# The gates of a DeltaNet layer: weights as the moving operand, tokens as the stationary one

## The chip, the cores and the metric

The kernel runs on one core of a Trainium2 chip. Its time is that of one execution on the device in microseconds; the median of the runs is compared. Below, PE is TensorE (matmuls; PEld is the loading of its stationary operand), DVE is VectorE, ACT is ScalarE, POOL is GpSimd and SP is the queue that issues the DMAs.

## What is computed

Two decoder layers on 1024 tokens of 1024 channels, in float32. The first has a gated DeltaNet as its token mixer, the second a convolution module; behind each is an MLP. Only the start of the DeltaNet matters here:

```python
proj = h @ w_in                                   # h: 1024 tokens x 1024; w_in: 1024 x 4112
qkv, z, bt, at = split(proj, [3072, 4096, 4104])  # bt, at: 8 columns each, one a head
qkv = silu(causal_depthwise_conv(qkv, conv_w))
beta = sigmoid(bt)
g = -exp(a_log) * softplus(at + dt_bias)
o = gated_delta_rule(l2norm(q), l2norm(k), v, g, beta)   # chunks, head by head
```

The gates bt and at are 16 columns of 4112. Everything in the delta rule waits for them: beta scales the Gram matrix of the keys, the running sum of g gives every decay.

## The kernel before

**Precision.** A float32 matmul is made of three in the faster fp32r format: each operand is split into a high part, rounded by a cast, and a low part, the rest. `mm3` issues high x high, high x low and low x high into one PSUM bank. A weight tile `raw` of 128x1024 is loaded by SP, its high part `whi` is cast on ACT (line 412, 225 in the first stage), its low part `wlo` is subtracted on DVE (line 415, 227). The input h is kept as H[half][k]: high and low part of 128 channels (block k) by 512 tokens (a half).

**A dense tile.** 128 output channels by 512 tokens: for each of 8 blocks of channels `mm3` takes a 128x128 weight block as the stationary operand and 512 tokens as the moving one, so 24 matmuls of 512 columns (lines 234 to 236). Tokens end up along the free axis.

**The first stage** (lines 287 to 305) fills all eight PSUM banks at once for the first half of the tokens, while the vectors of the conditioning are still being computed: for each k, h's block is made and multiplied by eight weight tiles from one load of 1024 columns, `w_first`. Bank 0 is the gates, padded from 16 to 128 columns with zeros; banks 1 to 7 are k, q, v of head 0, k, q, v of head 1 and k of head 2. The engines' order here is left to the framework's scheduler.

**The order behind it is written by hand.** For PE, DVE and ACT each piece of work is a generator, and a list of numbers says at which time (in slots, one a head, about 29 us) each of its steps is emitted. All steps are sorted by these times, and each of the three engines runs its instructions strictly in that order; a step that waits holds all behind it on its engine. POOL and SP are ordered by the scheduler. A weight tile's load, cast and subtraction get their times from the tile ahead of it: `tile_events` takes three times from the list `last` and leaves three for the next tile.

**The gates.** `token_gates(0)` takes bank 0: ACT copies 16 rows of it (line 354), four transposes (line 358) bring tokens onto the partitions, and DVE and ACT compute beta and the decays; two small products with a triangle give the running sums (lines 388, 389), one row a head goes to DRAM and comes back broadcast over all partitions. The second half's gates are a dense tile of their own in slot 7: 512 KB of weights loaded, cast and subtracted, 24 matmuls between times 7.0 and 7.2, then the same steps.

**PSUM.** In this part there are two banks for each of four tags: pd (dense tiles), pp (small products of a head's preparation and of the gates), pi (inverse), ps (scan). Who takes a bank with a tag waits until one is free, that is until all readers of the tile in it have run.

**What runs around time 7.** The steps of one head u are at fixed offsets:

- `head_prep` at u + 1: transposes of k into a pp bank at -0.0922 (line 493); ACT squares them at -0.0063 (line 496); the Gram product takes a pp bank at 0.0109 (line 501); DVE reads that at 0.1551 (line 512, writes NT); ACT reads the transposes again at 0.1822 (line 522, writes kd); the transposes of q take a pp bank at 0.2501 (line 527).
- `head_decay` at u: the exponentials of the decay on ACT at 1.1256 (lines 476, 477).
- `head_scan` at u + 3: a product on PE at 0.0646 (line 678), its reader on DVE at 0.0737 (line 681), then PE at 0.1923 (lines 685 to 689).
- `conv`, behind a projection tile: ACT copies and scales at 0.04 (lines 434, 439), three DVE steps (line 442), SiLU on ACT (line 445).

So at time 7 head 6 is in preparation and head 4 begins its scan.

Of the kernel before, what the change touches and what calls it, by code (L numbers as in the profile page):

```python
# [9 lines left out]
F32 = mybir.dt.float32  # L10
# [6 lines left out]
P = 128  # L17
D = 1024
# [37 lines left out]
DNO_AT = 0.0843  # L56
OG_AT = 4.8655
LATE_AT = (18.6148, 20.1732)
G0_AT = (-1.8, -1.7, -0.06, -0.01, 0.09, 0.25, 0.62, 0.645, 0.7, 0.72)
FIRST_AT = (  # L60
    (-1.6, -0.165, -0.12, -0.07, 0.1), (-1.2, -0.012, 0.03, 0.08, 0.11), (-0.02, 0.13, 0.175, 0.2, 0.27),
    (0.13, 0.49, 0.51, 0.53, 0.58), (0.25, 0.6, 0.65, 0.7, 0.74), (0.57, 0.75, 0.8, 0.85, 0.9),
# [1 line left out]
)  # L64
W_FIRST = ((-2.3, -1.95, -1.9),)
H0_AT = (0.8992, 1.98, 2.4218, 2.6956, 3.874, 4.2736, 6.2935, 6.8047)
G1_AT = (-0.0095, 0.088, 0.1601, 0.2135, 0.3241, 0.487, 0.7341, 0.7578, 1.2185, 1.3557)
PLAN = {
    0: (0, 3, ()), 1: (4, 1, ()), 2: (1, 2, ()), 3: (0, 2, ()), 4: (3, 0, ()), 5: (3, 0, ()), 7: (4, 0, ()), 8:
    (4, 0, ()), 14: (2, 1, ()), 15: (2, 1, ()), 16: (0, 2, ()), 17: (0, 2, (3,)), 18: (0, 0, (6, 0, 4, 7, 1)),  # L70
# [53 lines left out]
def tile_hybrid(ctx, tc, xT, c, adaT, cols, rows, gates, w_gate, w_first, w_dn, w_dno, w_cf, w_cfo,  # L124
# [39 lines left out]
    def bank(tag):  # L164
        return banks["pool"].tile([P, HALF], F32, name=nm(tag), tag=tag, bufs=banks[tag])
# [3 lines left out]
    def blk(j):  # L169
        return slice(j * P, (j + 1) * P)  # L170
# [16 lines left out]

    def raw_tile(ap):
        raw = wb("raw", 1024)
        nc.sync.dma_start(raw, ap)  # L190
        return raw

    def ada(l, j, k, raw=None):
# [27 lines left out]

    def load_w(ap):
        raw = raw_tile(ap)
        hi = wb("whi", 1024, F32R)
        sc.copy(hi, raw)
        lo = wb("wlo", 1024, F32R)
        ve.tensor_tensor(lo, raw, hi.bitcast(F32), op=ALU.subtract)
        return hi, lo

    def mm3(ps, w, off, acts, first=True, last=True):  # L230
# [53 lines left out]


    sb = Bufs("start", raw=6, tz=6)
    first = [bank(t) for t in ("pd", "pd", "pp", "pp", "pi", "pi", "ps", "ps")]
    for k in range(KT):
        ada(0, 1, k, sb("raw", D))
        ada(0, 0, k, sb("raw", D))  # L290
# [44 lines left out]
    gp.memset(W64, 0.0)  # L335
    beta, gam, negam, kdec, gdr = {}, {}, {}, {}, {}

    def v3(t):
        return t.rearrange("p (c m) -> p c m", m=P)

# [5 lines left out]

    def token_gates(hf):

        if hf == 0:
            ps = first[0]  # L350
        else:
            ps = yield
        gt = hb("tz")
        sc.copy(gt[0:16, :], ps[0:16, :])
        yield
        gps = bank("pp")
        for j in range(NC2):
            te.transpose(gps[:, j * 16:(j + 1) * 16], gt[0:16, blk(j)], ident[0:16, 0:16])
        yield
        gv = gps[:, 0:64].rearrange("p (c t h) -> p t h c", t=2, h=NH)  # L360

        def tile_(name):
            return dp(f"{name}{hf}", [NH, NC2])

        b_, gx, gy, gz, gq, gcol = [tile_(n) for n in ("beta", "gx", "gy", "gz", "gq", "gcol")]
        ve.tensor_tensor(gx, gv[:, 1], gate_c[:, 1, :].unsqueeze(2).broadcast_to(GS), op=ALU.add)
        yield

        sc.activation(gy, gx, AF.Abs)
        sc.activation(gy, gy, AF.Exp, scale=-1.0)  # L370
        sc.activation(b_, gv[:, 0], AF.Sigmoid)
        yield
        ve.tensor_scalar(gz, gy, 2.0, None, op0=ALU.add)
        yield
        ve.reciprocal(gz, gz)
        ve.tensor_mul(gy, gy, gz)
        ve.tensor_mul(gz, gy, gy)
        ve.tensor_scalar(gq, gz, 2.0 / 19.0, None, op0=ALU.mult)
        for t_ in range(17, 1, -2):
            ve.scalar_tensor_tensor(gq, gq, 2.0 / t_, gz, op0=ALU.add, op1=ALU.mult)  # L380
        ve.scalar_tensor_tensor(gq, gq, 2.0, gy, op0=ALU.add, op1=ALU.mult)
        ve.scalar_tensor_tensor(gq, gx, 0.0, gq, op0=ALU.max, op1=ALU.add)
        ve.tensor_tensor(gcol, gq, nea.unsqueeze(2).broadcast_to(GS), op=ALU.mult)
        yield

        n = NH * NC2
        ps = bank("pp")
        te.matmul(ps[:, 0:n], lhsT=kc[:, K_TRI, :], rhs=flat(gcol), start=True, stop=True)
        te.matmul(ps[:, n:2 * n], lhsT=kc[:, K_STR, :], rhs=flat(gcol), start=True, stop=True)
        yield  # L390
        gm, ng, kd = [tile_(x) for x in ("gam", "negam", "kdec")]
        ve.tensor_copy(flat(gm), ps[:, 0:n])
        sc.activation(flat(kd), ps[:, n:2 * n], AF.Exp)
        sc.activation(ng, gm, AF.Exp)
        yield
        ve.tensor_scalar(ng, ng, -1.0, None, op0=ALU.mult)
        ps = bank("pp")
        te.transpose(ps[0:n, 0:P], flat(gm), ident)
        yield
        grow = dp("grow", P, p=n)  # L400
        ve.tensor_copy(grow, ps[0:n, 0:P])
        d = dr.tile([NH, HALF], F32, name=nm("gdr"))
        nc.sync.dma_start(d.rearrange("h (c p) -> (h c) p", p=P), grow)
        beta[hf], gam[hf], negam[hf], kdec[hf], gdr[hf] = b_, gm, ng, kd, d
        yield
# [321 lines left out]
    def add(lab, g, *times):  # L727
        for t_ in times:
            events.append((t_, len(events), lab, g))
# [25 lines left out]
        tile_events(f"z{hf}", w_dn[24 + h], hf, t0, dur, lambda d: z_out(d, h, hf), Z_AT)  # L755

    def gate_events(t0, dur):
        g = token_gates(1)
        d = {}

        def post(d):
            g.send(None)
            g.send(d["ps"])
            yield
            yield from g

        tile_events("gates1", w_gate, 1, t0, dur, post, *G1_AT)

    def x_new(k):
        need("h", 0, k, n=2)  # L770
# [12 lines left out]
    order[6:12] = [(2, "k"), (2, "q"), (3, "k"), (3, "q"), (2, "v"), (3, "v")]  # L783
    for i, (u, t_) in enumerate(order[:7]):
        nt = {"q": 0, "k": 8, "v": 16}[t_] + u % NH
        add(f"proj0{u}", conv({"ps": first[1 + i]}, nt, 0, t_, heads[u]), *FIRST_AT[i])
    plan = {t_: PLAN.get(t_, (3, 0 if t_ < 12 else 1, ())) for t_ in range(19)}
    done = 7
    zs = 0
# [460 lines left out]
def layout(x, c, ada_w, ada_b, ln_g, ln_b, dn_w_in, dn_conv_w, dn_a_log, dn_dt_bias,  # L1250
           dn_norm_w, dn_w_out, cf_w_in, cf_dw_w, cf_dw_b, cf_ln_g, cf_ln_b, cf_w_out, ff_w1, ff_w2):
    cols = np.concatenate([
        _cols(ada_b), _cols(ln_g), _cols(ln_b),
        dn_conv_w[0].reshape(CONV, 24, P).transpose(2, 1, 0).reshape(P, 96),
        dn_norm_w[0][:, None],
        cf_dw_w[0].reshape(CFK, KT, P).transpose(2, 1, 0).reshape(P, KT * CFK),
        _cols(cf_dw_b), _cols(cf_ln_g), _cols(cf_ln_b)], axis=1)
    wg = np.zeros((D, P), np.float32)
    wg[:, :16] = dn_w_in[0][:, 4096:4112]
    return {  # L1260
        "xT": x[0].T.reshape(KT, P, S),
        "c": c,
        "adaT": ada_w.transpose(0, 2, 1).reshape(2, 48, P, D),
        "cols": cols,
        "rows": np.stack([ln_g[1, 1], ln_b[1, 1]]),
        "gates": np.stack([dn_a_log[0], dn_dt_bias[0]]),
        "w_gate": _wtiles(wg)[0],
        "w_first": np.concatenate([wg] + [dn_w_in[0][:, n * P:(n + 1) * P] for n in (8, 0, 16, 9, 1, 17, 10)],
                                  axis=1).reshape(KT, P, 1024),
        "w_dn": _wtiles(dn_w_in[0][:, :4096]),  # L1270
        "w_dno": _wtiles(dn_w_out[0]),
        "w_cf": _wtiles(cf_w_in[0]),
        "w_cfo": _wtiles(cf_w_out[0]),
        "w_1": np.stack([_wtiles(w) for w in ff_w1]),
        "w_2": ff_w2.reshape(2, 8, 4, P, 4, 2, P).transpose(0, 1, 4, 3, 5, 2, 6).reshape(2, 8, 4, P, 1024),
        "consts": _consts(),
    }
# [18 lines left out]
```

## Time and profile before

| | us |
|---|---|
| median of 3 runs (lowest, highest) | 2411.41 (2410.13, 2414.36) |
| the profiled execution | 2410.48 |
| its span in the profile | 2408.6 |
| first stage, until the gates' transposes | 57.35 |
| gates' tile of the second half | 254.97 to 260.78 |

The span is that of the instructions; the execution's own time has 1.9 us around it. A record of PE is longer than the time until the next one starts, since matmuls are pipelined: the pace is read from the starts. The granted clock of PE is 1.00 at 2.4 GHz and 0.50 at 1.2 GHz.

### The profile page before, as it was taken

Reading aid. Unit: us, or ns where it says so; the run is one execution under the profiler, and the core shown is the slowest. Engines: PE = TensorE matmul, PEld = TensorE weight load, DVE = VectorE, ACT = ScalarE, POOL = GpSimd, SP = SyncE. Lnnn points to the kernel's source line nnn. Section 1 sums busy time; section 2 is a strip of 40 time slices with the busy share of each in tenths; the row PEclk is TensorE's granted clock in tenths of the full one; section 3 lists DMA queues with packets and bytes.
Section 4 is the critical chain, followed back from the end, with each engine's and each line's share of the span. In section 5 each row is a group of like instructions: output and inputs, shape, how many; then the busy total and the mean of one; then the engine's idle time right before and its main releaser. Section 6 shows DMA issues by size and latency. Waiting matters only on the chain.

```text
span 2408.6 us, 33443 instructions
## 1 busy us (share of the span) xinstructions
PE 2357.5 (98%) x12730; PEld 1946.2 (81%) x12730; DVE 1722.9 (72%) x2712; ACT 1100.3 (46%) x1949; POOL 409.3 (17%) x841
## 2 busy tenths in 40 slices
PE   8899999999999999999999999999999999999998
PEld 6677878787778888888888888878888888888887
DVE  6667677676686566656899998799888766444447
ACT  4767767564256333335433334563333336333333
POOL 1356556454410000000000001100000001000003
PEclk9999999999999999999999999999999999999999
DMA  8343223334553556542322222222222332222223
GB/s 303 107 131 100 87 66 86 102 102 137 188 159 104 171 186 197 191 155 88 105 97 96 97 96 96 97 97 104 97 96 96 101 118 97 96 97 96 96 97 131
DMA packets 118143, 287.02 MB, mean 119 GB/s; under 512 B 35168, under 2 KB 44768, under 8 KB 117984
## 3 DMA queue, kind: packets, MB, share of 16 engines
q1 hardware_dynamic: 117984, 284.90, 36.3%
q8 instruction: 100, 1.64, 0.3%
q14 instruction: 59, 0.48, 0.1%
HBM read 275.35 MB, written 9.50 MB: 118 GB/s over the span
## 4 chain that ended last, share of the span: by engine, by line
PE 80%; DVE 7%; POOL 5%; DMA 4%; ACT 2%; issue 2%; SPq 0%; DVEq 0%; ACTq 0%; POOLq 0%
PE pd L234 25%; PE pd L236 25%; PE pd L235 24%; POOL T L563 2%; POOL X L565 2%; PE pp L982 1%; DVE wlo L415 1%; DVE tl L1031 1%; DVE lo L246 1%; DVE tl L1033 1%; DMA A<-d_in 1%; DMA d_in<-NT 1%; DMA Xc<-d_out 1%; DVE ax L259 1%; DVE raw L202 1%
## 5 line engine op out<-in xcount | busy, mean ns | idle before, releaser
L234 PE MATMUL pd<-hh,whi 128*128 128x512 f32 x2014 | 817.9, 406 | 6.9 <-DVE ax L259 3.9
L236 PE MATMUL pd<-hh,wlo 128*128 128x512 f32 x2014 | 789.5, 392 | 1.9 <-DVE wlo L415 1.8
L235 PE MATMUL pd<-lo,whi 128*128 128x512 f32 x2014 | 788.4, 391 | 0.6 <-DVE lo L246 0.6
L412 ACT CAST whi<-raw 128x1024 fp32r<-128x1024 f32 x382 | 398.4, 1043 | 544.5 <-PE pd L235 535.1
L415 DVE TENSOR_TENSOR wlo<-raw,whi 128x1024 fp32r<-128x1024 f32 x382 | 468.1, 1226 | 25.9 <-ACT whi L412 23.6
L236 PEld LDWEIGHTS pd<-hh,wlo 128*128 128x128 f32 x2014 | 379.6, 189 | 85.8 <-DVE wlo L415 4.7
L234 PEld LDWEIGHTS pd<-hh,whi 128*128 128x128 f32 x2014 | 381.4, 189 | 78.7 <-issue 3.9
L235 PEld LDWEIGHTS pd<-lo,whi 128*128 128x128 f32 x2014 | 381.6, 189 | 69.7 <-DVE lo L246 1.8
L234 PE MATMUL pd<-xh,whi 128*128 128x512 f32 (+1 forms) x1056 | 404.9, 383 | 0.0
L235 PE MATMUL pd<-xl,whi 128*128 128x512 f32 (+1 forms) x1056 | 404.1, 383 | 0.3 <-DVE xl L246 0.3
L236 PE MATMUL pd<-xh,wlo 128*128 128x512 f32 (+1 forms) x1056 | 404.1, 383 | 0.0
L961 DVE SCALAR_TENSOR_TENSOR cv<-u,col,cv 128x512 f32<-128x512 f32 x480 | 359.1, 749 | 9.6 <-ACT cv L957 1.8
L259 DVE SCALAR_TENSOR_TENSOR ax<-pd,mod,ax 128x512 f32<-128x512 f32 x280 | 208.4, 749 | 154.0 <-PE pd L236 152.9
L246 DVE TENSOR_TENSOR xl<-ts,xh 128x512 fp32r<-128x512 f32 x128 | 88.4, 691 | 256.6 <-ACT ts L905 256.0
L899 ACT ACTIVATE tz<-pd 128x512 f32<-128x512 f32 x128 | 76.6, 599 | 394.9 <-PE pd L236 394.9
L235 PEld LDWEIGHTS pd<-xl,whi 128*128 128x128 f32 x1056 | 198.5, 188 | 39.3 <-DVE xl L246 0.5
L234 PEld LDWEIGHTS pd<-xh,whi 128*128 128x128 f32 x1056 | 198.6, 188 | 38.6
L236 PEld LDWEIGHTS pd<-xh,wlo 128*128 128x128 f32 x1056 | 198.5, 188 | 38.5
L202 DVE CUSTOM_DVE_ANT_0 raw<-raw,condb 128x1024 f32<-128x1024 f32 x96 | 117.9, 1229 | 24.1 <-DMA raw<-in_adaT_dram 23.9
L563 POOL TENSOR_TENSOR T<-X,A 32x15 f32<-32x15 f32 (+7 forms) x240 | 100.1, 417 | 23.9 <-DMA A<-d_in 5.8
L565 POOL TENSOR_TENSOR X<-X,T 32x15 f32<-32x15 f32 (+7 forms) x240 | 99.1, 413 | 18.3
L991 POOL TENSOR_SCALAR lnst<-mv 128x1 f32<-128x1 f32 x32 | 14.9, 465 | 508.6 <-DVE mv L990 338.7
(248 smaller groups left out, 2177.5 us busy)
## 6 DMA issues: line engine op xcount, KB each, us to landing
raw<-in_w_dram SPq DMA_DIRECT2D x260, 512.0 KB, 3.2
raw<-in_adaT_dram SPq DMA_DIRECT2D x96, 512.0 KB, 3.4
raw<-in_w_dn_dram SPq DMA_DIRECT2D x57, 512.0 KB, 3.8
raw<-in_w_cf_dram SPq DMA_DIRECT2D x32, 512.0 KB, 3.2
raw<-in_w_dno_dram SPq DMA_DIRECT2D x16, 512.0 KB, 3.3
raw<-in_w_cfo_dram SPq DMA_DIRECT2D x16, 512.0 KB, 3.2
raw<-in_w_first_dram SPq DMA_DIRECT2D x8, 512.0 KB, 6.5
tz<-in_xT_dram SPq DMA_DIRECT2D x16, 256.0 KB, 5.5
```

The costliest lines, as they stand in the source:

```text
L202: ve.tensor_tensor_reduce(out=raw, in0=raw, in1=condb, op0=ALU.mult, op1=ALU.add, scale=1.0, scalar=0.0, accum_out=mod[l][j][:, k:k + 1])
L234: te.matmul(ps, lhsT=w[0][:, s_], rhs=ah, start=(first and i == 0), stop=False)
L235: te.matmul(ps, lhsT=w[0][:, s_], rhs=al, start=False, stop=False)
L236: te.matmul(ps, lhsT=w[1][:, s_], rhs=ah, start=False, stop=(last and i == n - 1))
L246: ve.tensor_tensor(lo, x32, hi.bitcast(F32), op=ALU.subtract)
L259: ve.scalar_tensor_tensor(AX[hf][k], ps, g[:, k:k + 1], AX[hf][k], op0=ALU.mult, op1=ALU.add)
L412: sc.copy(hi, raw)
L415: ve.tensor_tensor(lo, raw, hi.bitcast(F32), op=ALU.subtract)
L563: gp.tensor_tensor(t, X[:, 0:i + 1, i:i + 1].broadcast_to(sh), A[:, i:i + 1, i + 1:].broadcast_to(sh), op=ALU.mult)
L565: gp.tensor_tensor(X[:, 0:i + 1, i + 1:], X[:, 0:i + 1, i + 1:], t, op=ALU.subtract)
L899: sc.activation(r, d[0], AF.Relu)
L961: ve.scalar_tensor_tensor(cv, u[:, j:j + HALF], col[:, b_ + j:b_ + j + 1], cv, op0=ALU.mult, op1=ALU.add)
```

## The change

The gates' products are turned round: 128 tokens of h are the stationary operand, and the 16 weight columns of the gates the moving one. For each of four blocks of tokens and each of eight blocks of channels there are two products: h's high part with 32 columns (high and low weights side by side), and h's low part with the 16 high columns. That is 64 narrow products a half, into one bank of which 128 columns are used; tokens come out on the partitions, so the transposes go. ACT copies the one half of the columns to SBUF, and DVE adds the other. The weights (64 KB) are loaded, cast and subtracted once, behind the first stage.

The first stage fills seven banks from loads of 896 columns. Its narrow products for the first half stand at -0.013 to -0.01, ahead of the first dense tile, into a ps bank. Those of the second half stand at 7.06, 7.10, 7.14 and 7.18, into a pp bank; the dense tile in slot 7 is gone, and the slot is still divided by five. The gates' Exp and Sigmoid in the first half move from -0.01 to 0.11, behind the SiLU of head 0's k (0.10) and q (0.11).

```diff
-G0_AT = (-1.8, -1.7, -0.06, -0.01, 0.09, 0.25, 0.62, 0.645, 0.7, 0.72)
+G0_AT = (-0.013, -0.012, -0.011, -0.01, 0.1, 0.11, 0.16, 0.25, 0.62, 0.645, 0.7, 0.72)
-G1_AT = (-0.0095, 0.088, 0.1601, 0.2135, 0.3241, 0.487, 0.7341, 0.7578, 1.2185, 1.3557)
+G1_AT = (-0.14, -0.1, -0.06, -0.02, 0.03, 0.08, 0.2, 0.3241, 0.7341, 0.7578, 1.2185, 1.3557)
...
-    first = [bank(t) for t in ("pd", "pd", "pp", "pp", "pi", "pi", "ps", "ps")]
+    first = [bank(t) for t in ("pd", "pd", "pp", "pp", "pi", "pi", "ps")]
...
+    wg, raw_g = dp("wg", [KT, 32], F32R), hb("tz")
+    nc.sync.dma_start(raw_g[:, 0:P], w_gate)
+    raw_g = raw_g[:, 0:P].rearrange("p (k n) -> p k n", k=KT)
+    sc.copy(wg[:, :, 0:16], raw_g)
+    ve.tensor_tensor(wg[:, :, 16:32], raw_g, wg[:, :, 0:16].bitcast(F32), op=ALU.subtract)
...
     def token_gates(hf):
-        if hf == 0:
-            ps = first[0]
-        else:
-            ps = yield
-        gt = hb("tz")
-        sc.copy(gt[0:16, :], ps[0:16, :])
-        yield
-        gps = bank("pp")
-        for j in range(NC2):
-            te.transpose(gps[:, j * 16:(j + 1) * 16], gt[0:16, blk(j)], ident[0:16, 0:16])
-        yield
-        gv = gps[:, 0:64].rearrange("p (c t h) -> p t h c", t=2, h=NH)
+        gps = bank("pp" if hf else "ps")
+        for j in range(NC2):
+            for k in range(KT):
+                need("h", hf, k, n=1)
+                hi, lo = H[hf][k]
+                te.matmul(gps[:, j * 32:(j + 1) * 32], lhsT=hi[:, blk(j)], rhs=wg[:, k], start=(k == 0), stop=False)
+                te.matmul(gps[:, j * 32:j * 32 + 16], lhsT=lo[:, blk(j)], rhs=wg[:, k, 0:16], start=False,
+                          stop=(k == KT - 1))
+            yield
+        gs = dp("gs", [NC2, 16])
+        gv = gps[:, 0:NC2 * 32].rearrange("p (c n) -> p c n", c=NC2)
+        sc.copy(gs, gv[:, :, 16:32])
+        ve.tensor_tensor(gs, gs, gv[:, :, 0:16], op=ALU.add)
+        gv = gs.rearrange("p c (t h) -> p t h c", t=2)
...
     def gate_events(t0, dur):
-        g = token_gates(1)
-        d = {}
-
-        def post(d):
-            g.send(None)
-            g.send(d["ps"])
-            yield
-            yield from g
-
-        tile_events("gates1", w_gate, 1, t0, dur, post, *G1_AT)
+        add("gates1", token_gates(1), *[t0 + dur + o for o in G1_AT])
...
-        add(f"proj0{u}", conv({"ps": first[1 + i]}, nt, 0, t_, heads[u]), *FIRST_AT[i])
+        add(f"proj0{u}", conv({"ps": first[i]}, nt, 0, t_, heads[u]), *FIRST_AT[i])
```

`load_w` and `raw_tile` take tiles narrower than 1024 columns, and the host lays out the 16 gate columns alone and seven tiles in `w_first`.

## Rows read from the trace of the kernel before

**Rows 1.** The page, busy time of the engines, share of the span, instructions.
```profile
PE 2357.5 (98%) x12730; PEld 1946.2 (81%) x12730; DVE 1722.9 (72%) x2712; ACT 1100.3 (46%) x1949; POOL 409.3 (17%) x841
```
**Rows 2.** Windows: stretch, length, busy of PE, PEld, DVE, ACT, POOL, clock, DMA.
```profile
250.00:300.00 50.00, 48.85 (x368) 39.91 (x367) 33.26 (x82) 35.74 (x90) 23.78 (x59) 1.00 0.34 102
300.00:350.00 50.00, 47.16 (x426) 37.76 (x425) 39.23 (x85) 34.31 (x95) 27.04 (x55) 1.00 0.27 79
...
800.00:900.00 100.00, 100.00 (x443) 82.84 (x442) 64.38 (x100) 37.02 (x51) 0.57 (x3) 1.00 0.58 190
```
**Rows 3.** Timeline of PE, 254 to 262 us: start, duration, instruction, idle before.
```profile
254.16 1.06 PE L501 MATMUL pp<-k 128*128 128x128 f32 x8
254.97 0.48 PE L234 MATMUL pd<-hh,whi 128*128 128x512 f32 x1
...
257.11 0.38 PE L678 MATMUL ps<-lo,ax 128*128 128x128 f32 x2
...
260.78 0.38 PE L685 MATMUL ps<-vt,ax 128*128 128x128 f32 x2
```
**Rows 4.** Timeline of PE, 57 to 58.6 us.
```profile
57.35 0.41 PE L358 MATMUL pp<-ident,tz 16*128 16x16 f32 x4
57.69 0.50 PE L234 MATMUL pd<-hh,whi 128*128 128x512 f32 x1
```
**Rows 5.** Timeline of PE, 134.9 to 140 us.
```profile
136.02 1.00 PE L642 MATMUL pi<-V64T,NT 128*128 128x64 f32 x8
136.83 0.48 PE L234 MATMUL pd<-hh,whi 128*128 128x512 f32 x1
```
**Rows 6.** Timeline of PE, 292 to 297 us.
```profile
293.58 0.31 PE L388 MATMUL pp<-gcol,kcl 128*128 128x32 f32 x2
...
293.94 0.48 PE L234 MATMUL pd<-hh,whi 128*128 128x512 f32 x1
```
**Rows 7.** Timeline of DVE, 44 to 56 us.
```profile
50.44 1.23 DVE L227 TENSOR_TENSOR wlo<-raw,whi 128x1024 fp32r<-128x1024 f32 x1 [0.25 <-ACT whi L225]
```
**Rows 8.** Timeline of all engines, 60 to 115 us: TensorE.
```profile
65.35 0.74 PE L234 MATMUL pd<-hh,whi 128*128 128x512 f32 x1 [1.91 <-ACT whi L412]
...
68.49 0.57 PE L234 MATMUL pd<-hh,whi 128*128 128x512 f32 x1
```
**Rows 9.** Timeline of ACT, 50 to 66 us.
```profile
59.37 1.28 ACT L371 ACT_TABLE_LOAD   x1
```
**Rows 10.** Timeline of DVE, 253 to 264 us.
```profile
257.53 0.35 DVE L681 TENSOR_SCALAR vt<-ps,br 128x128 f32<-128x128 f32 x1 [4.56 <-PE ps L678]
...
261.49 1.13 DVE L512 SCALAR_TENSOR_TENSOR NT<-pp,br,ax 128x128 f32<-128x128 f32 x4
```
**Rows 11.** Waits of PE: who waited for whom, total, times, longest.
```profile
PE pp L527 <- DVE NT L512: 1.2, 2, 0.7
```
**Rows 12.** Timeline of ACT, 253.5 to 264 us.
```profile
254.98 0.73 ACT L439 ACTIVATE v<-pd,col 128x512 f32<-128x512 f32 x1
258.46 1.06 ACT L412 CAST whi<-raw 128x1024 fp32r<-128x1024 f32 x1 [2.75 <-DMA raw<-in_w_dn_dram]
259.53 1.28 ACT L476 ACT_TABLE_LOAD   x1
...
261.88 1.12 ACT L522 ACTIVATE ax<-pp,kdec 128x128 f32<-128x128 f32 x4
```
**Rows 13.** Windows of PE: stretch, length, busy, granted clock, DMA.
```profile
120.50:126.50 6.00, 5.98 (x76) 0.50 0.44 119
```
**Rows 14.** Timeline of PE, 108 to 128 us.
```profile
120.52 0.65 PE L598 MATMUL pi<-Tb,NT 32*32 32x32 f32 x32 [2.52 <-DVE Tb L583]
```
**Rows 15.** Timeline of PE, 698 to 714 us.
```profile
707.30 1.91 PE L982 MATMUL pp<-ident,ax 128*128 128x128 f32 x8
...
712.48 1.03 PE L982 MATMUL pp<-ident,ax 128*128 128x128 f32 x8
```
**Rows 16.** Groups of instructions of the whole span: busy, mean ns, idle before.
```profile
L234 PEld LDWEIGHTS pd<-hh,whi 128*128 128x128 f32 x2014 | 381.4, 189 | 78.7 <-issue 3.9 <-ACT whi L412 3.6 <-ACT whi L225 1.2
```

More of the change, by code (lines that the diff above doesn't have):

```diff
@@ L189, in raw_tile @@
         raw = wb("raw", 1024)
-        nc.sync.dma_start(raw, ap)
+        nc.sync.dma_start(raw[:, 0:ap.shape[-1]], ap)
         return raw
@@ L223, in load_w @@
         raw = raw_tile(ap)
+        n = ap.shape[-1]
         hi = wb("whi", 1024, F32R)
-        sc.copy(hi, raw)
+        sc.copy(hi[:, 0:n], raw[:, 0:n])
         lo = wb("wlo", 1024, F32R)
-        ve.tensor_tensor(lo, raw, hi.bitcast(F32), op=ALU.subtract)
+        ve.tensor_tensor(lo[:, 0:n], raw[:, 0:n], hi[:, 0:n].bitcast(F32), op=ALU.subtract)
         return hi, lo
@@ L1257, in layout @@
         _cols(cf_dw_b), _cols(cf_ln_g), _cols(cf_ln_b)], axis=1)
-    wg = np.zeros((D, P), np.float32)
-    wg[:, :16] = dn_w_in[0][:, 4096:4112]
     return {
@@ L1266, in layout @@
         "gates": np.stack([dn_a_log[0], dn_dt_bias[0]]),
-        "w_gate": _wtiles(wg)[0],
-        "w_first": np.concatenate([wg] + [dn_w_in[0][:, n * P:(n + 1) * P] for n in (8, 0, 16, 9, 1, 17, 10)],
-                                  axis=1).reshape(KT, P, 1024),
+        "w_gate": dn_w_in[0][:, 4096:4112].reshape(KT, P, 16).transpose(1, 0, 2).reshape(P, P),
+        "w_first": np.concatenate([dn_w_in[0][:, n * P:(n + 1) * P] for n in (8, 0, 16, 9, 1, 17, 10)],
+                                  axis=1).reshape(KT, P, 7 * P),
         "w_dn": _wtiles(dn_w_in[0][:, :4096]),
```

## The prediction

> **What bounds the kernel now.** I read the page first. TensorE is busy for almost the whole span [rows 1]. Its record overstates it (matmuls are pipelined), so the second view is busy time by stretches: after the DeltaNet part TensorE has no gap at all, while in the DeltaNet part VectorE and ScalarE are at two thirds to four fifths and TensorE has 1 to 3 us of gap in 50 us [rows 2]. The reader is to see that a microsecond of TensorE work added or taken in the DeltaNet part mostly reaches the end, because the engines run in a written order and everything behind moves with it; only a gap that lies behind the change can swallow some. The third view is the timeline at the two places where the gates are computed: the end of the first stage (50 to 72 us) and slot 7 (254 to 266 us).
>
> **What the change takes away.** The first stage loses one bank of eight: 8 blocks of 3 products. The gates' tile of the second half is the same 24 products: in slot 7 they stand between 254.97 and 260.78, with the two short products of line 678 among them, 5.8 us in all, or 0.23 us a product [rows 3]. So 5.5 us of TensorE work go from each place, and with them the four transposes, 0.34 us (57.35 to 57.69) [rows 4].
>
> **What it adds.** 64 products a half, each with its own 128x128 stationary tile and 32 or 16 moving columns. No row has this form in fp32r. The nearest: eight products of line 642 (64 columns, full stationary tile) run from 136.02 to 136.83, 0.101 us each [rows 5]; four with 32 columns from 293.58 to 293.94, 0.09 us each [rows 6]; four transposes with 16 columns on 16 rows in 0.34 us, 0.085 us each [rows 4]. A quarter fewer columns change little, so the loading of the stationary tile sets the pace and not the columns. I take 0.10 us: 6.4 us a half (5.4 at 0.085; 6.9 at 0.107, were the load alone a little slower). Against 5.8 us with the transposes this is +0.6 us a half. The narrow form does not save TensorE work.
>
> The Trainium skill (TensorE: Matmul & The Clock Gate, section Back-to-back issue gap) gives about 81 ns for a sustained pair of load and matmul at 128 columns; by it the 64 would take some 5.2 us, an estimate. The eight of line 642 run at 101 ns here, so the row is used. The same page (Part 3, The mechanism) says that a weight load overlaps a running matmul only if the row groups differ; by that 64 products would take a load and a stream each.
>
> **Place 1, the first stage and gates0.** The stage ends today at 57.35 [rows 4], behind a backlog of products. Without 5.5 us of them it would end at 51.8; VectorE's last low part ends at 51.67 [rows 7], is an eighth shorter in each of eight blocks (0.15 us of 1.23, so 1.2 us earlier in all: 50.5), and seven products of 0.23 us follow: 52.1. From there 6.4 us of narrow products give 58.5, so the first dense tile starts 0.8 us later than at 57.69. What follows is set by ScalarE: the second tile waits 1.91 us for its cast and then runs at the lower clock until 68.5 [rows 8]. The evacuations of the seven banks move forward under the narrow products and shorten that wait. But the gates' Exp and Sigmoid now stand behind the SiLU of head 0's k and q, where they stood ahead of them: two more table loads of 1.28 us [rows 9]. Bounds: the wait and its slow stretch vanish, -1.9 and -1.5 us (half of the 3.1 us that were slow); or nothing of it vanishes and the delay and both loads land on the path, 0.8 + 2.6 = +3.4 us. I take 0, for both sides are as large.
>
> The narrower casts, the half megabyte less in the first loads and the 64 KB of the gates' weights cost nothing that I count: they lie under the stage's products. If the cover goes, the copy and subtraction of the small weights are two instructions of 128 elements a row, some 0.35 us each by line 681 [rows 10].
>
> **Place 2, slot 7.** Here the order changes. The four blocks of narrow products stand at 7.06, 7.10, 7.14 and 7.18, and the first takes a bank with the tag pp, of which there are two. At 7.06 both are held by the preparation of head 6: the bank of the k transposes (taken at 6.908, read last by line 522 at 7.182) and that of the Gram product (line 501 at 7.011, read by line 512 at 7.155). That such a hold stops TensorE shows in the wait of line 527 for line 512, the reader of the bank before it [rows 11]. Which of the two comes free first? Line 512 stands on VectorE behind line 681 at 7.074, and that waits for line 678 at 7.065, which now stands behind the narrow products on TensorE [rows 10]. So VectorE can't free one, and line 522 on ScalarE must. ScalarE ends the convolution's copies at 255.71; it then waited 2.75 us for a weight tile and cast it, the tile after the gates' [rows 12]. In the changed order that tile takes over the early load and cast of the gates' tile (the list of times handed from tile to tile has one member less), so ScalarE goes on at once: table load, two exponentials, line 522, which took from 259.53 to 263.00, 3.47 us [rows 12]. The bank is free at about 259.2. TensorE has done line 501 at 254.97 and has nothing in between, for the dense tile that stood there is gone: it stands still for 4.2 us. Then 6.4 us of narrow products and the 0.14 us of line 678 end at 265.75, where line 685 now starts at 260.78 [rows 3]: +5.0 us. Queued behind: lines 678, 681, 512, hence head 6's solve, and the next dense tiles.
>
> A stop of that length has a second price. After a stop of 2.52 us the granted clock stood at 0.50, the lower level of 1.2 GHz, for 6.0 us [rows 13, 14]; after the one of 1.91 us products ran slow for 3.1 us [rows 8]. That costs half of it with dense products behind, 1.5 to 3 us. Here narrow ones follow; eight transposes took 1.91 us at the lower level and 1.03 at the higher [rows 15], so if all 64 run slow it is about 0.8 x 6.4 = 5.1 us, and 3 us more for dense ones behind. I take 3 us, with 0 and 8 as ends.
>
> The gates' load of 512 KB, its cast and its subtraction leave SP, ScalarE and VectorE in this slot. I count nothing for it: TensorE, which waits for none of them there today, is what ends last. Of the gaps behind the place, 2.8 us between 300 and 350 [rows 2], some may swallow a little; I take none off.
>
> **Sum.** 0 + 5.0 + 3 = +8 us. The profiled execution took 2410.48 us, 1.9 us more than its span, and the median of the runs is 0.9 us above it. On the execution 2418.5; on the runs 2419.
>
> **The rivals.**
> *The bank is not late.* If ScalarE is far enough ahead, or the reader of the other bank goes first, only the added work is left, 2 x 0.6 us, and place 1: +1 to +3 us, 2413. For it speaks that ScalarE sat idle for 2.75 us in this very place; against it that its chain to line 522 starts only when the preceding dense tile is done.
> *Faster.* The DeltaNet part hangs on the chain through ScalarE, VectorE and GpSimd, not on TensorE. That chain begins with the evacuation of the first stage's banks, and the stage ends at 52.1 in place of 57.35: everything behind comes 5.2 us earlier, and in slot 7 TensorE's stop is slack, since the chain waits for line 522 as before: -5.2 us, 2406. It decides if less than 0.4 us of the 5.2 is lost on the way, for 4.8 us are 0.2%. For it speaks that TensorE stood behind ScalarE at 65.35 [rows 8] and has gaps all through the part [rows 2]; against it that these gaps are only 1 to 3 us in 50.
> *The narrow runs are slow themselves.* TensorE falls to the lower clock in the narrow run of place 1 too, or each product pays load and stream one after the other: 64 x 0.08 = 5 us and 1.5 to 3 of dense ones behind it, on top of the forecast and with the whole 8 in slot 7: +8 + 5 + 5 = +18 us, 2429. No row shows a run of narrow products longer than 1 us, so nothing excludes the first. The second the Trainium skill's rule on overlap would bring; the trace speaks against it: a load is recorded with 0.19 us [rows 16], and line 642 starts a product each 0.101.
>
> **How the numbers follow.** The forecast has 0.55 (by itself 2414 to 2426), the bank that is not late 0.23, faster 0.09, the slow narrow runs 0.13. Of the forecast about a tenth falls within 0.2% (4.8 us, about what a measurement of this kernel tells from no change), because gaps behind may swallow part. Slower 0.62, the same 0.29, faster 0.09. The range is 2409 to 2428: it leaves out the faster case and the upper end of the slow runs.
>
> **What would show it.** Right: between line 501 of head 6 and the first narrow product TensorE is idle for some 4 us, released by ScalarE's line 522, with a granted clock near 0.5 just behind; the narrow products start 0.09 to 0.11 us apart at the full clock; the first stage ends near 52; the first dense tile starts at 58 to 59. Wrong: TensorE goes from line 501 straight into narrow products; or they stand 0.06 or 0.2 us apart; or the delay of slot 7 is gone again by 350 us, swallowed by gaps.

## The result: 0.8% slower, and the profile after

The changed kernel took 2432.0 us (median of 4 runs, 2426.4 to 2432.6) against 2412.2 us for the kernel before on the same chip: ratio 1.0079, 95% interval 1.0067 to 1.0091. The forecast was 2419, its range ended at 2428. Of the rivals, that of the slow narrow runs (2429) came nearest; how far its reasons hold is told further down. The profiled executions stand 21.1 us apart (2431.62 and 2410.48).

The page's busy times hide this: TensorE is busy for the same 98% as in [rows 1], with 72 instructions more and 13.9 us more busy time.

```profile
PE 2371.4 (98%) x12802; PEld 1961.5 (81%) x12802; DVE 1721.1 (71%) x2714; ACT 1098.4 (45%) x1949; POOL 407.8 (17%) x841
```

To see where the time went I lay one instruction that every head has once, the Gram products (line 501 before, 510 after), side by side in the two timelines. Head 0 starts 3.1 us later than before, head 6 4.1 us, head 7 18.3 us, head 15 22.3 us. So in these two executions the first place costs 3 to 4 us, slot 7 costs 14.2 us, and 3.3 us come between heads 8 and 9. Lines after the edit have moved: 234 is now 235, 501 is 510, 522 is 531, 678 is 687, 685 is 694; the narrow products are lines 361 (high part, 32 columns) and 362 (low part, 16).

Head 7's Gram products, first before, then after (head 6's are in [rows 3] and below):

```profile
296.08 1.06 PE L501 MATMUL pp<-k 128*128 128x128 f32 x8
```
```profile
314.39 1.05 PE L510 MATMUL pp<-k 128*128 128x128 f32 x8
```

The first place, timeline of TensorE in the kernel after: start, duration, instruction. It answers to [rows 4] and [rows 8].

```profile
52.83 0.39 PE L237 MATMUL ps<-hh,wlo 128*128 128x512 f32 x1
53.06 0.18 PE L361 MATMUL ps<-wg,hh 128*128 128x32 f32 x1
...
57.66 0.26 PE L361 MATMUL ps<-wg,hh 128*128 128x32 f32 x1
57.77 0.27 PE L362 MATMUL ps<-wg,lo 128*128 128x16 f32 x1
57.90 0.38 PE L361 MATMUL ps<-wg,hh 128*128 128x32 f32 x1
58.11 0.36 PE L362 MATMUL ps<-wg,lo 128*128 128x16 f32 x1
...
61.95 0.36 PE L362 MATMUL ps<-wg,lo 128*128 128x16 f32 x1
62.16 0.77 PE L235 MATMUL pd<-hh,whi 128*128 128x512 f32 x1
...
67.86 0.52 PE L236 MATMUL pd<-lo,whi 128*128 128x512 f32 x1
68.22 0.40 PE L237 MATMUL pd<-hh,wlo 128*128 128x512 f32 x1
```

No line here has a bracket, so TensorE waited for nothing. The products start 0.111 us apart until 57.77 and 0.213 us apart from 57.90: in the middle of the run, 4.8 us after its start, the clock fell to the lower level. The run took 9.1 us, and the dense products behind it stayed slow until 67.9. The windows say the same: full busy, granted clock 0.79, then 0.50 (1.2 GHz). Columns: stretch, length, TensorE busy, granted clock, DMA share and GB/s.

```profile
55.00:60.00 5.00, 5.00 (x38) 0.79 0.02 7
60.00:65.00 5.00, 5.00 (x18) 0.50 0.00 0
...
260.00:265.00 5.00, 1.68 (x8) 0.77 0.81 227
265.00:270.00 5.00, 5.00 (x25) 0.50 0.28 110
270.00:275.00 5.00, 5.00 (x25) 0.50 0.25 59
275.00:280.00 5.00, 5.00 (x51) 0.50 0.00 0
280.00:285.00 5.00, 5.00 (x20) 0.68 0.01 2
```

The lower five are slot 7: the clock is down for some 19 us. The timeline of TensorE there, beside [rows 3]:

```profile
258.24 1.06 PE L510 MATMUL pp<-k 128*128 128x128 f32 x8
263.32 0.40 PE L361 MATMUL pp<-wg,hh 128*128 128x32 f32 x1 [4.02 <-ACT ax L531]
263.56 0.36 PE L362 MATMUL pp<-wg,lo 128*128 128x16 f32 x1
...
266.76 0.77 PE L687 MATMUL ps<-lo,ax 128*128 128x128 f32 x2
...
277.42 0.77 PE L694 MATMUL ps<-vt,ax 128*128 128x128 f32 x2
...
279.14 0.80 PE L235 MATMUL pd<-hh,whi 128*128 128x512 f32 x1
...
283.39 0.40 PE L236 MATMUL pd<-lo,whi 128*128 128x512 f32 x1
```

The stop is in the bracket: 4.02 us, released by the copies that read the k transposes' bank. All 64 narrow products behind it stand 0.213 us apart, from 263.3 to 277.4, and the full rate is back only at 283.4, behind dense products. ScalarE went on without the wait of [rows 12], as the prediction had it, from line 448 into the table load:

```profile
259.06 0.72 ACT L448 ACTIVATE v<-pd,col 128x512 f32<-128x512 f32 x1
259.80 1.28 ACT L485 ACT_TABLE_LOAD   x1
...
262.15 1.12 ACT L531 ACTIVATE ax<-pp,kdec 128x128 f32<-128x128 f32 x4
```

### The profile page after: what moved, and what is told of

It is laid out like the page before. It is cut to its first block, busy times and chain, and to the rows that moved or that the text cites. A ratio compares the mean times of both kernels' runs of the same rounds, so it can differ in the third digit from the quotient of the medians.

```text
span 2429.7 us, 33585 instructions
## 1 busy us (share of the span) xinstructions
PE 2371.4 (98%) x12802; PEld 1961.5 (81%) x12802; DVE 1721.1 (71%) x2714; ACT 1098.4 (45%) x1949; POOL 407.8 (17%) x841
## 4 chain that ended last, share of the span: by engine, by line
PE 80%; DVE 8%; POOL 5%; DMA 3%; ACT 2%; issue 2%; SPq 0%; ACTq 0%; DVEq 0%; POOLq 0%
PE pd L235 24%; PE pd L237 24%; PE pd L236 24%; POOL T L572 2%; POOL X L574 2%; PE pp L982 1%; DVE wlo L424 1%; DVE raw L202 1%; DVE lo L247 1%; DMA Xc<-d_out 1%; DVE tl L1031 1%; DVE tl L1033 1%; DVE ax L260 1%; DMA raw<-in_adaT_dram 1%; PE ps L687 0%
## 5 line engine op out<-in xcount | busy, mean ns | idle before, releaser
L574 POOL TENSOR_TENSOR X<-X,T 32x15 f32<-32x15 f32 (+7 forms) x240 | 96.2, 401 | 18.3
```

The costliest lines, as they stand in the source:

```text
L574: gp.tensor_tensor(X[:, 0:i + 1, i + 1:], X[:, 0:i + 1, i + 1:], t, op=ALU.subtract)
```

## The experiments

Each kernel is compared with the kernel before on the same chip. That took 2410.9 us beside half0, half1, bank_pd and wide, 2411.4 beside wide_pd, mix, two and stop_dense, and 2413.4 beside wide_pd2 and two2. The table shows, for the profiled execution of each kernel, how much later than before the Gram products of head 0, head 6 and head 7 start, worked out from the timelines; the last column is the difference of the two before it, the price of slot 7 in that execution. The kernel half0, whose slot 7 is that of before, shows 1.2 us there: smaller differences say nothing. A profiled execution can lie some us off the median of its kernel (bank_pd 2427.2 against 2422.8, wide_pd2 2423.6 against 2418.3), and the changed kernel's began its products 0.8 us earlier than that of the kernel before. So the columns of head 0 and head 6 are rough; slot 7 is a difference within one execution, and after and half1, which have the same slot 7, agree in it (14.2 and 14.4).

| kernel | ratio to before, 95% | head 0 | head 6 | head 7 | slot 7 |
|---|---|---|---|---|---|
| after | 1.0079 (1.0067 to 1.0091) | +3.1 | +4.1 | +18.3 | 14.2 |
| half0 | 1.0028 (1.0016 to 1.0040) | +5.0 | +5.3 | +6.5 | 1.2 |
| half1 | 1.0061 (1.0046 to 1.0076) | +1.5 | +0.4 | +14.8 | 14.4 |
| bank_pd | 1.0054 (1.0039 to 1.0069) | +6.4 | +9.5 | +14.7 | 5.2 |
| wide | 1.0077 (1.0060 to 1.0094) | +2.6 | +5.4 | +18.1 | 12.7 |
| wide_pd | 1.0049 (1.0035 to 1.0064) | +2.3 | +5.4 | +14.4 | 9.0 |
| wide_pd2 | 1.0020 (1.0010 to 1.0030) | +2.7 | +6.6 | +10.4 | 3.8 |
| mix | 1.0046 (1.0032 to 1.0060) | +4.3 | +4.9 | +10.0 | 5.1 |
| stop_dense | 1.0059 (1.0045 to 1.0074) | +2.7 | +6.6 | +16.3 | 9.7 |
| two | 0.9994 (0.9980 to 1.0008) | +1.8 | +1.2 | -0.5 | -1.7 |
| two2 | 1.0007 (0.9998 to 1.0016) | +3.4 | +4.5 | +3.3 | -1.2 |

**One half at a time: half0 and half1.** The first turns round only the first half's products and keeps the dense gates' tile in slot 7; the second does the reverse.

```diff
-        gps = bank("pp" if hf else "ps")
-        ... 64 narrow products
+        if hf == 0:            # half1: if hf == 1
+            ... 64 narrow products
+        else:
+            ... the padded tile, copy and transposes of before
```

> Only the first half's gates are turned round (seven banks, narrow products behind the first stage); the second half keeps its dense tile. Theory A (the two places add up, and the clock falls inside the narrow run by itself): the lead of 3 to 4 us that the Gram products show between the two places stays, 2415 to 2417 us, and the granted clock falls to 0.50 some 4.8 us into the run. Rival B (the first place costs nothing by itself, the loss comes from slot 7 and what it drags along): 2411 to 2413 us.

> Only the second half's gates are turned round; first stage and first half as before. Theory A: the wait of 4 us for the bank and a run at the lower clock from its first product to its last, 64 x 0.213 = 13.6 us where the dense tile took 5.8: 2426 to 2430 us. Rival B (slot 7 is as bad as it is only because the first place had made everything late): below 2422 us.

half0 took 2418.1 us, half1 2424.8, each about 1 us outside the range of its theory A. That the halves add up holds within the noise: +7.2 and +14.0 are 21.2 against +19.8 for both. Theory B of half1, that slot 7 is dear only because the first place made it late, falls: its stop is there with head 6 only 0.4 us late, and slot 7 costs the same 14.4 us. The line from half1, TensorE:

```profile
259.65 0.40 PE L362 MATMUL pp<-wg,hh 128*128 128x32 f32 x1 [4.03 <-ACT ax L547]
```

In half0 the narrow run was at the lower clock from 57.2 us on, and its runs spread widely (2412.6 to 2423.4).

**The stop taken away: bank_pd.** The second half's products go into a pd bank, which is free.

```diff
-        gps = bank("pp" if hf else "ps")
+        gps = bank("pd" if hf else "ps")
```

> As changed, but the narrow products of slot 7 take a bank with the tag pd, of which one is free there, so the wait of 4 us goes. Theory A (the narrow run itself lowers the clock): the run starts at 0.11 us a product, falls to 0.21 some 5 us into it as in the first place, and a stretch of dense products behind is slow: it saves the 4 us and some 4 to 5 of slow products, 2422 to 2425 us. Rival C (the wait had lowered the clock, and without it the clock stays up): 64 x 0.111 = 7.1 us at the higher level, 2415 to 2419 us.

It took 2422.8 us: theory A. TensorE in slot 7:

```profile
263.63 1.06 PE L510 MATMUL pp<-k 128*128 128x128 f32 x8
264.45 0.26 PE L361 MATMUL pd<-wg,hh 128*128 128x32 f32 x1
...
268.80 0.26 PE L362 MATMUL pd<-wg,lo 128*128 128x16 f32 x1
268.92 0.38 PE L361 MATMUL pd<-wg,hh 128*128 128x32 f32 x1
...
276.18 0.80 PE L235 MATMUL pd<-hh,whi 128*128 128x512 f32 x1
...
279.61 0.48 PE L235 MATMUL pd<-hh,whi 128*128 128x512 f32 x1
```

The narrow products follow the Gram products without a gap at 0.111 us, and 4.5 us into the run, with no stop ahead, they double as in the first place. So the stop's share of slot 7 is 14.2 - 5.2 = 9.0 us: its own 4.0, some 38 products that are slow only because of it (38 x 0.102 = 3.9), and a rest of 1.1 in the work behind. The other 5.2 us are the run's own.

**The same products with 128 columns: wide, wide_pd, wide_pd2.** Each narrow product streams its 32 weight columns four times; this adds the product of the two low parts to the result, and the surplus columns are not read. wide keeps the changed kernel's bank, wide_pd takes the free one.

```diff
-                te.matmul(gps[:, j * 32:(j + 1) * 32], lhsT=hi[:, blk(j)], rhs=wg[:, k], ...)
-                te.matmul(gps[:, j * 32:j * 32 + 16], lhsT=lo[:, blk(j)], rhs=wg[:, k, 0:16], ...)
+                to, r4 = gps[:, blk(j)]..., wg[:, k].unsqueeze(1).broadcast_to([P, 4, 32])
+                te.matmul(to, lhsT=hi[:, blk(j)], rhs=r4, ...)
+                te.matmul(to, lhsT=lo[:, blk(j)], rhs=r4, ...)
```

> As changed, but each of the 64 products streams 128 columns: the 32 weight columns four times over, for the high and for the low part; the surplus results are not read (and the product of the two low parts is added). The pace at the higher clock should stay at 0.11 us a product if the load of the stationary tile sets it. Theory D (the clock falls because so few columns stream): in the first place the clock stays at 1.00, and in slot 7, where it falls with the wait, it comes back within the run: 2422 to 2426 us. Rival E (what counts is the small number of products or the loads, not the columns): as changed, 2430 to 2433 us.

> The changed kernel with both of its earlier edits: each narrow product streams 128 columns (the 32 weight columns four times; the product of the two low parts is added, and the surplus columns are not read), and the second half writes to a free pd bank, so that TensorE does not stand still before it. Theory A (the clock falls after a stop, and it falls without one where the runs stream few columns; 128 columns keep it): no stretch of lower clock from 55 to 70 us nor from 262 to 285 us; the second run takes 64 x 0.111 = 7.1 us against 24 x 0.227 = 5.4 us of the dense tile that it replaces, so +1.7 us there, and with the +2.6 to +5.4 us that the first place cost at 128 columns the median is 2414 to 2419 us. Theory B (128 columns kept the clock in the first place only because the dense stage lay right ahead of it; amid the shorter products of a head the run loses it): the clock falls at some 4.5 us into the second run as it did with the free bank alone, that place costs 5 us, median 2420 to 2424 us.

wide took 2428.7 us, between its theories. Its windows, the first place and slot 7:

```profile
55.00:60.00 5.00, 5.00 (x48) 1.00 0.28 96
60.00:65.00 5.00, 5.00 (x32) 1.00 0.00 0
...
265.00:270.00 5.00, 5.00 (x27) 0.51 0.46 168
...
275.00:280.00 5.00, 5.00 (x54) 0.50 0.07 7
```

In the first place the run of 128 columns, again 0.111 us a product, stays at the full clock from end to end, where that of 32 and 16 columns fell: the pace is the same with 16, 32 and 128 columns, the clock is not. In slot 7, behind the same stop (4.02 us), the clock falls all the same and does not come back within the run, so wide saved less than hoped there.

wide_pd has no stop ahead of either run, and its clock stays at 1.00 from 50 to 75 and from 252 to 285 us. It still took 2423.6 us. That lies in the range of theory B only by chance, for the fall of the clock in the second run that B counts on is not there: both theories missed the reason. Its timelines, first TensorE, then VectorE, then GpSimd; the last line is GpSimd in the kernel before:

```profile
280.50 0.39 PE L237 MATMUL pd<-hh,wlo 128*128 128x512 f32 x1
288.07 0.80 PE L682 MATMUL ps<-S,k 128*128 128x128 f32 x2 [7.18 <-DVE S L705]
```
```profile
271.40 0.15 DVE L717 SCALAR_TENSOR_TENSOR ss<-ss,eq 128x4 f32<-128x4 f32 x1
...
286.40 0.69 DVE L720 TENSOR_TENSOR o<-o,ss 128x512 f32<-128x512 f32 x1 [11.01 <-POOL ss L257]
```
```profile
285.36 1.01 POOL L257 TENSOR_TENSOR ss<-ss,expo 128x4 f32<-128x4 f32 x1
```
```profile
264.96 1.98 POOL L256 TENSOR_TENSOR ss<-ss,expo 128x4 f32<-128x4 f32 x1 [0.50 <-DVE ss L707]
```

VectorE waits 11 us for GpSimd's root of four numbers. GpSimd's order, unlike that of the other three, is not written out in this kernel, and here it has the root behind the whole block substitution of head 6 (273.1 to 285); in the kernel before it stands ahead of it (264.96), and so it does in the changed kernel (283.86) and in bank_pd (280.39). wide has the same late order (289.06), but VectorE waits only 2.72 us for it there, and TensorE not at all. wide_pd2 puts it back by making the substitution read the root:

```diff
         X = XX[:, 0]
+        if u == 6:
+            gp.tensor_copy(T[:, 0, 1:1 + NC2], heads[3]["ss"][0:32, :])
```

> 128 columns and the free bank again, with one more copy of four numbers on GpSimd, which makes the block substitution of head 6 wait for head 3's root mean square; nothing else differs. In the run without it GpSimd had that root behind the whole substitution of head 6 (VectorE waited 11.01 us for it, TensorE 7.18 us for VectorE), where the kernel before has it ahead. Theory A (that wait, not the narrow run, was the price of slot 7 in the run without the copy): the 7.18 us wait and the lower clock from 285 to 291 us behind it are gone, slot 7 costs 1.5 to 3 us instead of 9.0, median 2415 to 2418 us. Theory B (the narrow run delays the chains of slot 7 by itself, and the root was only what came last): another wait of 4 us or more takes its place, median 2421 to 2425 us.

2418.3 us with the kernel before at 2413.4: the 7.18 us wait is gone, slot 7 costs 3.8 us instead of 9.0. Theory A in the main, though not down to its 1.5 to 3 us: a wait of 1.95 us for a weight tile's low part (line 425) is left, behind the gates' chain on VectorE, and behind that wait the clock is at the lower level for some 3 us (289 to 292.4). TensorE's timeline and its window:

```profile
287.15 0.50 PE L237 MATMUL pd<-hh,wlo 128*128 128x512 f32 x1 [1.95 <-DVE wlo L425]
```
```profile
290.00:292.50 2.50, 2.50 (x10) 0.51 0.12 26
```

So +4.9 us is what the turned-round products still cost with 128 columns when the stop is gone and both runs keep the clock. Part of it is that wait and its slow stretch; no run shows the price without them.

**Narrow products between dense ones: mix.** The 64 products of a half are cut into 16 blocks of four; two blocks stand between two dense groups in the first place, one in slot 7. Same arithmetic.

```diff
-G0_AT = (-0.013, -0.012, -0.011, -0.01, 0.1, 0.11, ...)
+G0_AT = tuple((i // 2 + 0.5) / 24 + 0.01 * (1 + i % 2) for i in range(16)) + (0.34, 0.345, ...)
...
+                if k % 2:
+                    yield
```

> The changed kernel with the 64 narrow products of each half cut into 16 blocks of four (two k, high and low), one or two of them behind each group of three dense products: in the first place among the eight groups of the first z tile, in the second spread over slot 7, whose hole for the gates is taken out; the second half's bank is asked for when it has long been free. Same arithmetic, same number of products. Theory A (it is the closed run of narrow products, not the products, that brings the clock down): no stretch of lower clock at either place, pace 0.111 us inside the blocks, 64 x 0.111 = 7.1 us per half against 5.4 us of the dense tile: +1.7 us per half, and 1 to 2 us more for the first stage's waits for its weight tiles, median 2414 to 2417 us. Theory B (narrow products cost the clock wherever they lie): half clock through the blocks and the dense groups between them, +8 to +10 us per half, median 2424 to 2430 us. Theory C (a block of small products between dense groups breaks into TensorE's flow, each switch costs 0.1 us or more): 32 blocks, +3 us on top of A, median 2417 to 2421 us.

2424.5 us. On the clock theory A is right: at both places no stretch below 1.00 while the blocks ran. In the first place the pattern is clean, eight narrow products in 0.81 us, a dense group in 0.79:

```profile
53.93 0.18 PE L361 MATMUL ps<-wg,hh 128*128 128x32 f32 x1
...
54.74 0.49 PE L235 MATMUL pd<-hh,whi 128*128 128x512 f32 x1
...
55.53 0.18 PE L361 MATMUL ps<-wg,hh 128*128 128x32 f32 x1
...
65.86 0.47 PE L235 MATMUL pd<-hh,whi 128*128 128x512 f32 x1
...
72.38 0.41 PE L398 MATMUL pp<-gcol,kcl 128*128 128x32 f32 x2 [1.47 <-DVE gcol L393]
```

On the time it is wrong; the median lies in the range of theory B, but not for B's reason. What costs here are my times for the gates' chain, which this kernel sets later: the last row waits 1.47 us for it and the clock falls soon after (0.80 from 72.5 to 75 us, 0.50 from 75 to 80), and head 7 waits 1.45 us for the second half's chain. As a price of mixing the run's time is inconclusive. The trace of the first place is not: the sixteen blocks and the seven dense groups between them take 11.93 us (53.93 to 65.86), against 64 x 0.111 + 21 x 0.227 = 11.87. A switch has no price that shows, so theory C falls there.

**A stop with dense products behind: stop_dense.** half0, with the padded tile's 24 products of slot 7 put where the narrow run stood, in a pp bank.

```diff
+            ps = bank("pp")
+            for j in range(KT):
+                mm3(ps, d["w"], j * P, [H[1][j]], j == 0, j == KT - 1)
...
+        add("gates1", mm(), *[t0 + dur + o for o in (-0.14, -0.1, -0.06, -0.02)])
```

> The first half as in the changed kernel; in slot 7 the kernel before's 24 dense products with the padded weight tile, but put where the changed kernel has its narrow run and into a pp bank, so that TensorE meets the same stop of 4 us ahead of them. Theory A (the stop brings the clock down whatever follows, but what streams after it decides when it comes back): a wait of 4 us on ACT ax, half clock for 5 to 8 us from 262 us on (not 20), the products at 0.43 us in it; slot 7 costs 4 us of stop and 2.5 to 4 us of clock, so 6.5 to 8 us where the narrow run cost 14; with the first half alone at 2418 us, median 2424 to 2426 us. Theory B (the time at the lower clock after a stop is the same whatever follows): half clock for 15 to 20 us, slot 7 costs 12 us or more, median over 2428 us. Theory C (the stop costs nothing but its own length): no stretch of lower clock there, median 2421 to 2422.5 us.

2426.5 us, as theory A, but by another sum: the gates' tile takes the early load again, so ScalarE waits 2.78 us for the weight tile behind it, as in [rows 12], and casts it (1.04 us) before it comes to the copies. The stop is 7.83 us and not 4.

```profile
269.67 0.79 PE L235 MATMUL pp<-hh,whi 128*128 128x512 f32 x1 [7.83 <-ACT ax L548]
...
273.68 0.41 PE L237 MATMUL pp<-hh,wlo 128*128 128x512 f32 x1
```

After a stop almost twice as long the dense products are at full rate 4.0 us after they begin; ten products ran slow (two of them line 704's), 2 us lost: 7.8 + 2 = 9.8 against 9.7 measured. The narrow run of the changed kernel was still slow 14 us after it began.

**The other way to save columns: two and two2.** The gate weights stay the stationary operand, 32 columns wide, and the tokens stream 512 columns at a time: 16 products a half instead of 24 or 64, and no padded tile to load. two2 also takes a free bank for the first half's transposes.

```diff
+    def gate_mm(ps, hf, k):
+        hi, lo = H[hf][k]
+        te.matmul(ps[0:32, :], lhsT=wg[:, k], rhs=hi, start=(k == 0), stop=False)
+        te.matmul(ps[0:16, :], lhsT=wg[:, k, 0:16], rhs=lo, start=False, stop=(k == KT - 1))
...
+        gps = bank("pp" if hf else "pd")      # two2; two: bank("pp")
```

> Neither kernel's form: the gate weights stay the stationary operand, but 32 columns wide (16 high, 16 low), and the tokens stream 512 columns at a time, so two products per k where the kernel before has three and the changed kernel has eight; the 512 KB load of the padded tile is gone, the first stage has seven weight tiles and a bank for the gates. Theory A (TensorE sets the pace in both places and long streams keep the clock): 8 products of 0.227 us fewer per half, -3.6 us in all, of which waits of the shorter first stage for its weight tiles take back 0.5 to 1.5 us: median 2407 to 2410 us with the kernel before at 2411. Theory B (the chain through ScalarE, VectorE and GpSimd sets the pace, so a shorter tile on TensorE gives nothing): 2411 +- 1.5 us. Theory C (a seven-tile first stage is starved of weight tiles by all that it saves and more): the first Gram product of head 0 comes later than in the kernel before, 2412 to 2415 us.

> The kernel with 32 stationary columns and 512 moving ones, with the first half's transposes into a pd bank that is free in place of a pp bank that ScalarE still reads. In the run without this TensorE waited 2.77 us there (ACT q) and the clock was at 0.5 to 0.8 from 57.5 to 62.5 us. Theory A (TensorE sets the pace at that place): wait and lower clock gone, 3 to 4 us earlier at the first Gram product of head 0, median 2406 to 2409 us, ratio 0.997 to 0.9985 to the kernel before. Theory B (the chains of head 0 through ScalarE, VectorE and the weight tiles set the pace there): the wait moves to the next weight tile, median 2410 to 2412 us, no difference that can be measured.

2410.5 against 2411.4 us, and 2415.3 against 2413.4: neither is to be told from the kernel before, theory B for both. Of the 1.8 us that TensorE saves in each half, slot 7 shows 1.2 to 1.7 in the table, little more than the 1.2 that half0 shows without a change there; in the first place it came to nothing. There the wait went from the transposes (two, 2.77 us on ScalarE) to the next weight tile (two2). First TensorE, then ScalarE of two2:

```profile
67.82 0.80 PE L235 MATMUL pd<-hh,whi 128*128 128x512 f32 x1 [4.36 <-ACT whi L437]
```
```profile
66.14 0.69 ACT L464 ACTIVATE k<-pi,col 128x512 f32<-128x512 f32 x1
66.72 1.04 ACT L437 CAST whi<-raw 128x1024 fp32r<-128x1024 f32 x1
```

The cast stands at the end of an unbroken row of ScalarE's work that starts at 60.19, behind a wait of 1.40 us for VectorE. So in the first place the next tile starts when ScalarE gets to its cast, and 1.8 us less on TensorE gained nothing.

## Why the prediction was wrong, point by point

*Right.* The bank is late: 4.02 us against 4.2, released by line 522's counterpart, with ScalarE going on without the wait for a weight tile. The pace at the full clock is 0.111 us, just above the bounds of 0.085 to 0.107: 7.1 us a half where 6.4 were taken. The first stage ends at 53.06 (52.1); in it are 1.9 us of waits for its own weight tiles (0.19 before), for which the prediction had counted nothing. The wait of 1.91 us [rows 8] is gone. The Trainium skill's 81 ns for a load and product pair (TensorE: Matmul & The Clock Gate, section Back-to-back issue gap) is not what this form does here: 111 ns.

*The step that failed: "That costs half of it with dense products behind ... I take 3 us, with 0 and 8 as ends."* The mechanism was named and mis-sized by a factor of three. From the Gram products to line 685 slot 7 took 6.62 us before and 19.18 after, 12.6 more; the prediction's +5.0 and the run at 0.213 in place of 0.10 us (64 x 0.113 = 7.2) make 12.2 of it. The dense products behind bring the place to 14.2, so the second price is 9.2 us. Of that, 0.7 us is the pace (0.111 in place of 0.10) and 8.5 the clock, of which the run itself has 64 x 0.102 = 6.5; the other end of the bounds, 8, was nearer than the 3 that I took. I had sized it by rows in which dense products followed the stop, and stop_dense shows that they were read rightly for those: 2 us. What failed was the choice between the two cases in the same paragraph; here narrow ones followed, and they did not bring the clock back.

*The term of the first place, "I take 0", stood on 6.4 us for the run.* It took 9.1, because the clock fell inside it without any stop. That was the first half of the rival of the slow narrow runs, given 0.13 since no row showed a narrow run longer than 1 us. bank_pd and wide show it for what it is: the same fall without a stop in slot 7, and none with 128 columns at the same pace. The second half of that rival, that a product pays load and stream one after the other, is refuted: 16, 32 and 128 columns all go at 0.111. The arithmetic of the first place holds otherwise: 58.5 + 0.95 for the stage + 2.7 for the run = 62.15, and the first dense tile starts at 62.16. Of the 4.5 us by which that is late, 1.4 are made up by head 0. That rival's price for a slow run, 64 x 0.08 us, stands on no row; the runs show 0.102 us more a product. Its 2429 came near in part by luck: it had 5 us in the first place (3 to 4 in the trace), 13 in slot 7 (14.2) and nothing between heads 8 and 9 (3.3).

*The rival "faster"* finds no support in two and two2: 1.8 us less on TensorE at the first place did not get past ScalarE's row. *The bank that is not late* was bank_pd: even then the change costs 0.5%.

*Not forecast:* 3.3 us between heads 8 and 9, where the changed kernel ran at the lower clock from about 358 to 365 us. half0, half1 (355 to 358.5), wide, wide_pd, mix and two2 have such a stretch near there; the kernel before, bank_pd, wide_pd2, stop_dense and two have none. The waits ahead of it (0.88, 0.56 and 1.05 us between 354 and 360 us) are almost those of the kernel before (0.88, 0.56 and 1.11 between 335 and 341 us), which keeps its clock there. A further wait ahead of them is longer than before (1.03 us against 0.19), but wide_pd2 has it too (0.91) and keeps its clock. So these waits alone do not explain it, and the cause stays open.

The Trainium skill (TensorE: Matmul & The Clock Gate, section HAM oscillation) explains a falling clock by waits between products. The trace agrees in slot 7 (4.02 us, then 0.50) and not in the first place, where TensorE was busy for 5.00 of 5.00 us and the clock fell.

## What to carry to other kernels

Before swapping operands to save moving columns, count the stationary tiles: at 0.111 us each, 64 narrow products cost 7.1 us where 24 full streams cost 5.4. A closed run of narrow products also lost the clock here 2.8 to 5.4 us after its start and did not bring it back; blocks of it between dense groups, or wider streams, kept it. Before putting work at a new place in a written order, look up which bank it takes and who reads that bank last: a single letter of a tag was worth 9 us in the traces (8 in the medians, +19.8 against +11.9).

## What the runs showed of the hardware that was not expected

- A narrow run lowered TensorE's clock without a pause: 4.8 us (after), 3.5 (half0), 2.8 (bank_pd) and 5.4 (stop_dense) after its start in the first place, 4.5 us in slot 7 (bank_pd). The same number of products with 128 columns, at the same 0.111 us, kept it.
- Once down, the clock stayed down through 64 narrow products, of 32 and 16 columns (14.1 us) and of 128 (265.1 to 278.3, wide). Dense products of 512 columns brought it back between 2.3 us (wide, 279.98 to 282.25) and 6.1 us (after, first place, 62.16 to 68.22) after they began.
- The first product of an execution started between 10.27 us (after) and 11.82 us (wide_pd2) in kernels with the same first stage; differences below 1.5 us in the first place cannot be told from that spread.
- GpSimd's order moved with edits that touch no GpSimd instruction: in wide and wide_pd a root of four numbers went behind 12 us of other work, and in wide_pd that cost TensorE 7.18 us.
